# Layer B's scores of a pair of heads in one run of matmuls, in a two-layer attention encoder

## The chip, the cores and the metric

The kernel runs on one core of one Trainium2 chip. The metric is the device time of one execution, in microseconds; lower is better. TensorE is called PE here, VectorE DVE, ScalarE ACT, GpSimd POOL, and the queue of SyncE, which issues nearly all transfers, SP.

## The reference

Two layers work on 512 tokens of width 1024, in float32. Each layer normalises its input, projects it (q, k, v and a gate), attends with 16 heads of 64, multiplies by the SiLU of the gate, projects back and adds the input. Layer A is a dilated sliding-window attention; layer B, the one that the change touches, attends over a grid of 8 rows by 64 columns:

```python
def mixer_b(hn, w_in, w_out, q_gain, k_gain, rpb):
    proj = hn @ w_in
    q, k, v, gate = jnp.split(proj, 4, axis=-1)
    q = rms_norm(q.reshape(b, s, N_HEADS, HEAD_DIM), q_gain) * (HEAD_DIM ** -0.5)
    k = rms_norm(k.reshape(b, s, N_HEADS, HEAD_DIM), k_gain)
    ...
    def row(r):                      # one of 8 grid rows; 4 blocks of 16 columns
        ...
        logits = jnp.einsum('bhcqd,bhrcjd->bhcqrj', qr, kr).astype(jnp.float32) + bias
        logits = jnp.where(col_valid[:, :, None, :], logits, NEG_INF)
        p = jax.nn.softmax(logits.reshape(b, N_HEADS, n_cb, NA_COL_BLOCK, wr * NA_SLAB), axis=-1)
        ...
        out = jnp.einsum('bhcqrj,bhrcjd->bhcqd', p, vr)
    ...
    y = y * jax.nn.silu(gate)
    return y @ w_out
```

A query sees the keys of all rows in a slab of columns around its own. Each layer's output is added to its input.

## The kernel before

**Main work and side work.** PE's order is written out by hand. `main()` is a generator of the projections: weights stream in from memory, 512 KB at a time (`wraw`, three buffers, loaded by SP at L184), are split by ACT (`wh`, L132) and by DVE or POOL (`wl`, L138) into two parts of a reduced float32 type, and each product is made of three matmuls (high by high, high by low, low by high) of 512 columns into a PSUM bank of `acc` (four banks, `ps_acc`). `side()` is a second generator: attention, head pair by head pair. `run` takes a step of the main work (three matmuls, mostly), then lets the side work go on if it is due. What is due is kept on a clock of the kernel's own, which is counted as the program is written out, not on the chip: `matmul` adds 213 for 512 columns, so a step of three is 640; a transposition of 128 columns adds 109. `yield 1200` in the side work means "go on once the clock has gone 1200 further"; `later_on(9000, job)` puts a job in the program at the first step that is 9000 or more later. PE follows this order; ACT, DVE, POOL and SP are ordered by a scheduler that follows the program's order and a simulated timeline, except where `keep_in_program_order` pins an instruction. Instructions wait for each other's data by semaphores.

**The order of layer B's main work** is a list of parts: q and k of two pairs of heads at a time ("qk", moved by DVE and ACT into `raw` when a projection ends, L485), v of four pairs at a time ("v", into `rawk`, L485), and gates of one pair each. A "qk" or "v" part takes 96 full matmuls and needs all four `acc` banks, a gate 24 and one bank.

**Layer B's side work, `side_b(hc)`,** is done for eight pairs of heads (hc, or pair, 0 to 7). It asks for PSUM banks from a second pool of four (`bank`, `ps_side`), in turn:

1. For pairs 2 to 7, the P·V product of the pair before last (`pending`, `weigh`, tile `o`), whose P has been on its way through memory.
2. Bias rows for a later pair (`bias_b`, SP L748 and L753, tile `eb`, two buffers).
3. q transposed on PE (bank `tp`), split into `qh` and `ql`; 2500 of the clock later k, split into `kh` (ACT, L661) and `kl` (DVE, L665).
4. 1750 later the scores. There are four blocks of 128 queries against 256 keys. `scores(u)` does two of them, u = 0 and then u = 1, into two banks `log`, one for each head of the pair: per block three products for each head. A head has 64 channels, so a matmul uses 64 of PE's 128 rows, and the two heads' matmuls go in pairs side by side. One call is 12 matmuls of 256 columns.
5. `softmax(hd, u, lg)` for each head and half: DVE adds the bias and takes the minimum (L1109; scores are kept negated) from `log` into `p`, ACT takes the exponential and its sum (L1119), DVE the reciprocal (L693), ACT scales (L694). The small tile `mn`, which carries minimum and sum, has four buffers; a call of `softmax` uses two, one for each block, from the minimum to the scaling.
6. P is transposed. For pairs 0 to 5 (`far`) DVE transposes squares of 32 (L770, tile `tr`); then SP writes `tr` to memory (`td<-tr`, L779) and reads it back in four parts, rearranged (`pt<-td`, L783). `turner.send` is called through `later_on` some time after the transpositions, and puts the four reads on the clock itself: 9500 after the send, and then 1200 apart. For pairs 6 and 7 PE transposes P in four turns 1000 apart, and `weigh` follows at once.

Between `scores(0)` with its softmax and `scores(1)` there is `yield 1200`, in which PE does main work.

Of the kernel before, what the change touches and what calls it, by code (L numbers as in the profile page):

```python
# [46 lines left out]
def tile_hybrid_encoder(  # L47
# [23 lines left out]
    def sb(t, off, dims):  # L71
        return bass.AP(t.tensor, t.offset + off, [t.ap[0]] + dims)
# [13 lines left out]
    def bank(name):  # L86

        return ps_side.tile([P, 512], F32, tag="side", name=name)
# [137 lines left out]
    def mm3_heads(os, lh, ll, rh, rl, last):  # L226

        for n, (l, r) in enumerate(((lh, rh), (lh, rl), (ll, rh))):
            for hd in range(2):
                hs = slice(64 * hd, 64 * hd + 64)  # L230
                matmul(os[hd], l(hs), r(hs), share=2, start=(n == 0), stop=(last and n == 2))
# [3 lines left out]
    def later_on(delay, job):  # L235

        timers.append((clock[0] + delay, job))
        timers.sort(key=lambda t: t[0])
# [452 lines left out]
    def normalise(pr, mn):  # L691

        nc.vector.reciprocal(mn[:, 3:4], mn[:, 2:3])  # L693
        nc.scalar.activation(pr, pr, AF.Copy, scale=mn[:, 3:4])  # L694

    def put_y(hc, o, permuted, last):

        gt, rest = st.pop(("gate", hc))
        for _ in rest:
            pass  # L700
        if last and permuted:
            for c in range(4):
                q = slice(P * c, P * c + P)
                of = lambda t: t.rearrange("p (s x) -> p s x", x=16)[:, :, 4 * c : 4 * c + 4]
                nc.vector.tensor_mul(of(gt), of(gt), of(o))
                src = gt.rearrange("p (t ja x) -> p x ja t", t=4, ja=8)[:, 4 * c : 4 * c + 4]
                h, l = (t[:, hc, q].rearrange("p (x ja t) -> p x ja t", x=4, ja=8) for t in (st["y_h"], st["y_l"]))
                nc.scalar.copy(h, src)
                nc.vector.tensor_sub(l, src, h.bitcast(F32))
            return  # L710
        h, l, src = st["y_h"][:, hc, :], st["y_l"][:, hc, :], gt
        if permuted:

            tc.keep_in_program_order(nc.vector.tensor_mul(gt, gt, o))
            src = gt.rearrange("p (t ja x) -> p x ja t", t=4, ja=8)
            h, l = (t.rearrange("p (x ja t) -> p x ja t", t=4, ja=8) for t in (h, l))
        else:
            for grid, line in ((mid_rc, mid_o), (edge_rc, edge_o)):
                nc.vector.tensor_mul(grid(gt), grid(gt), line(o))
        nc.scalar.copy(h, src)  # L720
        (nc.vector if last else nc.gpsimd).tensor_sub(l, src, h.bitcast(F32))
        stamp["ya" if permuted else "yb", hc, "y"] = 0
# [327 lines left out]
    def side_b(hc):  # L1050
# [27 lines left out]
        pt, turners = pq[:, 2048 * (hc % 2) : 2048 * (hc % 2) + 2048], []  # L1078
# [1 line left out]
        at = lambda a, hd, i: 448 * a + 224 * hd + 32 * i  # L1080

        def scores(u):
            lgs = [bank("log") for _ in range(2)]
            for b in (2 * u, 2 * u + 1):
                if b < 3:
                    m = lambda t_, hs: t_[hs, P * b : P * b + 256]
                else:
                    m = lambda t_, hs: sb(t_[hs], 0, [[384, 2], [1, P]])
                qs = slice(P * b, P * b + P)
                o = 256 * (b % 2)  # L1090
                mm3_heads(
                    [lg[:, o : o + 256] for lg in lgs],
                    lambda hs: qh[hs, qs], lambda hs: ql[hs, qs], lambda hs: m(kh, hs), lambda hs: m(kl, hs), True,
                )
            return [(hd, u, softmax(hd, u, lgs[hd])) for hd in range(2)]

        def softmax(hd, u, lg):
            pr = wk.tile([P, 512], F32, tag="p", name="p", bufs=4)
            for b in (2 * u, 2 * u + 1):
                mn = wk.tile([P, 4], F32, tag="mn", name="mn", bufs=4)  # L1100
                o = 256 * (b % 2)
                if b < 3:
                    parts = ((slice(0, P), o),)
                    n, ec = 256, 0
                else:
                    parts = ((slice(0, 64), o), (slice(64, P), o + P))
                    n, ec = 128, 256
                for rows, c in parts:
                    nc.vector.tensor_tensor_reduce(  # L1109
                        out=pr[rows, o : o + n],  # L1110
                        in0=lg[rows, c : c + n],
                        in1=e[rows, hd, ec : ec + n],
                        scale=1.0,
                        scalar=3.0e38,
                        op0=ALU.add,
                        op1=ALU.min,
                        accum_out=mn[rows, 0:1],
                    )
                nc.scalar.activation(  # L1119
                    pr[:, o : o + n], pr[:, o : o + n], AF.Exp, bias=mn[:, 0:1], scale=-1.0, accum_out=mn[:, 2:3]  # L1120
                )
                normalise(pr[:, o : o + n], mn)
            return pr
# [9 lines left out]
        def weigh():  # L1133
            assert not any(t.left for t in turners)
            vb = st["vb", hc // 4]
            o = bank("o")
            mms = []


            for d, n, m, i, a in (  # L1140
                (64, 128, 0, 0, 0), (0, 64, 0, 6, 0), (192, 256, 2, 3, 0), (448, 64, 3, 6, 2),
                (64, 256, 1, 1, 0), (320, 128, 3, 5, 0),
            ):
                q = [[32, min(n // 32, 4)], [1, 32]]
                p = [[448, min(n // 32, 4)], [1, 32]]
                if n == 256:
                    q, p = [[P, 2]] + q, [[32, 2]] + p
                mms.append((
                    lambda t_, d=d, q=q: sb(t_, d, q),
                    lambda hs, m=m: vb[:, m, P * (hc % 4) + hs.start : P * (hc % 4) + hs.stop],  # L1150
                    lambda hd, p=p, i=i, a=a: sb(pt, at(a, hd, i), p),
                ))
            side_by_side(o, mms)
            return o

        held = []
        for u in range(2):
            held += scores(u)
            yield 1200 if u == 0 else 2400
        if far(hc):  # L1160
            turned = turner(448)
            turners.append(turned)
            for hd, u, pr in held:
                turned.put(pr, 512 if u == 0 else 384, 224 * hd + 128 * u)
            later_on(9000, partial(turned.send, pt[:, :1792], 9500, 1200))
            pending.append(lambda: put_y(hc, weigh(), False, False))
            return
        for args in held:
# [27 lines left out]
    def side():  # L1196
# [48 lines left out]
        for hc in range(NHC):  # L1245
            yield from side_b(hc)
# [100 lines left out]
```

## Time and profile before

| | |
|---|---|
| time, median of 3 runs | 845.8 us (845.26 to 847.01) |
| profiled execution, span | 843.7 us |
| profiled execution, a time of its own | not listed beside the span; the runs' median lies 2.1 us above it |
| granted TensorE clock | 1.000 |
| PE busy | 837.7 us, 5378 matmuls |
| DVE, ACT, POOL busy | 528.4, 427.8, 294.2 us |
| HBM | 109.11 MB read, 31.12 MB written |
| layer B's scores on PE | from 616.2 us to 802.8 us, 192 pairs of matmuls, 16 visits |

Rows of the timeline are: start in us, time in us, engine, line, operation, tile written `<-` tiles read, shapes, count, and in brackets how long the engine had been idle before it and what released it. Rows of the waits are: engine, what waited, `<-` for whom; total us, times, longest. Rows of the chain (the work that ended last, followed back) are: start in us, us, what. PEld is PE's loading of weights, which can run under a matmul. A matmul's time in a row includes its passage through the array; the pace is read from the starts. L215 is the line of the helper `matmul`, so the tile's name tells what is computed: `acc` the projections, `log` the scores, `tp` transpositions, `o` P·V.

### The profile page before, as it was taken

To read this page: it belongs to the slowest core of one execution; us is meant where nothing else is said; L and a number is where in the kernel's file an instruction comes from. 1 tells how busy PE (TensorE), PEld (TensorE's weight loads), DVE (VectorE), ACT (ScalarE), POOL (GpSimd) and SP (SyncE) were. 2 spreads that over 40 slices of the span, in tenths; PEclk is the share of its full clock that TensorE was granted. 3 is DMA by queue.
4 is the path that set the end of the run, shared out by engine and by line. 5 is a ranking of instruction groups with operands and counts; after the bars stand their busy time and mean duration, and the time that the engine had idled before them with its cause. 6 is when DMAs were issued, how large, how long until landed. Compare 5 with 4: busy or idle time off the path is not lost.

```text
span 843.7 us, 14965 instructions
## 1 busy us (share of the span) xinstructions
PE 837.7 (99%) x5378; PEld 676.3 (80%) x5378; DVE 528.4 (63%) x1371; ACT 427.8 (51%) x899; POOL 294.2 (35%) x432
## 2 busy tenths in 40 slices
PE   9999999999999999999999999999999999999998
PEld 7788888788788788788788787888878877777777
DVE  7354684684674674675674675447565777668653
ACT  7432653563553653652653564344366465664541
POOL 3352442452441541542532341121521625235211
PEclk9999999999999999999999999999999999999999
DMA  6345478378378278378276364164236546447323
GB/s 253 112 132 178 150 215 248 139 212 259 124 213 258 98 227 246 95 235 244 92 220 189 115 195 110 60 233 176 78 102 197 155 145 191 121 150 202 102 92 131
DMA packets 64218, 141.20 MB, mean 167 GB/s; under 512 B 5648, under 2 KB 23248, under 8 KB 64144
## 3 DMA queue, kind: packets, MB, share of 16 engines
q1 hardware_dynamic: 64000, 139.99, 54.0%
q8 instruction: 42, 0.69, 0.3%
q10 hardware_dynamic: 144, 0.26, 0.1%
q14 instruction: 32, 0.26, 0.1%
HBM read 109.11 MB, written 31.12 MB: 166 GB/s over the span
## 4 chain that ended last, share of the span: by engine, by line
PE 95%; DMA 2%; ACT 1%; DVE 1%; issue 0%; SPq 0%; ACTq 0%
PE acc L215 80%; PE log L215 5%; PE o L215 5%; PE tp L219 3%; DMA pt<-td 1%; DMA wraw<-in_w 1%; DVE hn_l L403 1%; ACT p L1119 1%; DMA x_all<-in_xt 0%; ACT p L694 0%; DVE pt L1017 0%; PE pa L215 0%; ACT raw L485 0%; PE pl L215 0%; PE pk L215 0%
## 5 line engine op out<-in xcount | busy, mean ns | idle before, releaser
L132 ACT CAST wh<-wraw 128x512 fp32r<-128x512 f32 (+1 forms) x259 | 158.3, 612 | 283.5 <-PE acc L215 246.0
L215 PE MATMUL acc<-wh,hn_h 128*128 128x512 f32 x704 | 282.4, 402 | 1.1 <-ACT hn_h L402 0.7
L215 PE MATMUL acc<-wh,hn_l 128*128 128x512 f32 x704 | 274.2, 390 | 0.0
L215 PE MATMUL acc<-wl,hn_h 128*128 128x512 f32 x704 | 274.1, 390 | 0.0
L138 POOL TENSOR_TENSOR wl<-wraw,wh 128x512 fp32r<-128x512 f32 (+1 forms) x104 | 135.2, 1300 | 366.1 <-ACT wh L132 344.5
L138 DVE TENSOR_TENSOR wl<-wraw,wh 128x512 fp32r<-128x512 f32 (+1 forms) x156 | 111.8, 717 | 146.4 <-ACT wh L132 145.3
L215 PEld LDWEIGHTS acc<-wh,hn_h 128*128 128x128 f32 x704 | 132.1, 188 | 35.8 <-issue 5.6
L215 PEld LDWEIGHTS acc<-wh,hn_l 128*128 128x128 f32 x704 | 132.2, 188 | 28.6
L215 PEld LDWEIGHTS acc<-wl,hn_h 128*128 128x128 f32 x704 | 132.4, 188 | 25.2 <-POOL wl L138 0.3
L215 PE MATMUL acc<-y,wh 128*128 128x512 f32 (+1 forms) x272 | 82.5, 387 | 0.0
L215 PE MATMUL acc<-hn_h,wh 128*128 128x512 f32 x192 | 76.1, 396 | 0.0
L215 PE MATMUL acc<-hn_h,wl 128*128 128x512 f32 x192 | 74.9, 390 | 0.0
L215 PE MATMUL acc<-hn_l,wh 128*128 128x512 f32 x192 | 74.8, 389 | 0.0
L694 ACT ACTIVATE p<-p,mn 128x512 f32<-128x512 f32 (+3 forms) x128 | 69.4, 585 | 0.6 <-DVE mn L693 0.2
L857 ACT ACTIVATE p<-p,mn 128x512 f32<-128x512 f32 (+1 forms) x64 | 44.8, 701 | 46.8 <-DVE mn L846 46.5
L291 DVE TENSOR_REDUCE ss<-sq 128x4 f32<-128x256 f32 (+1 forms) x96 | 48.3, 505 | 30.1 <-POOL sq L290 18.7
L770 DVE STREAM_TRANSPOSE tr<-p 128x512 f32<-128x512 f32 (+1 forms) x80 | 53.7, 683 | 12.3 <-ACT p L694 11.6
L215 PEld LDWEIGHTS acc<-y,wh 128*128 128x128 f32 x272 | 48.1, 189 | 9.6 <-issue 1.3
L215 PE MATMUL acc<-y,wl 128*128 128x512 f32 (+1 forms) x136 | 51.4, 378 | 0.0
L215 PEld LDWEIGHTS acc<-hn_h,wh 128*128 128x128 f32 x192 | 36.1, 188 | 8.0 <-issue 0.3
L215 PEld LDWEIGHTS acc<-hn_h,wl 128*128 128x128 f32 x192 | 36.0, 188 | 7.7
L215 PEld LDWEIGHTS acc<-hn_l,wh 128*128 128x128 f32 x192 | 36.1, 188 | 7.0
(143 smaller groups left out, 1041.1 us busy)
## 6 DMA issues: line engine op xcount, KB each, us to landing
wraw<-in_w SPq DMA_DIRECT2D x119, 512.0 KB
td<-tr SPq DMA_DIRECT2D x14, 1024.0 KB
pt<-td SPq DMA_DIRECT2D x56, 256.0 KB
qd<-rawq SPq DMA_DIRECT2D x6, 1024.0 KB
qt<-qd SPq DMA_DIRECT2D x24, 256.0 KB
td<-tr SPq DMA_DIRECT2D x6, 896.0 KB
pt<-td SPq DMA_DIRECT2D x24, 224.0 KB
e<-l_d SPq DMA_DIRECT2D x32, 112.0 KB
```

The costliest lines, as they stand in the source:

```text
L132: nc.scalar.copy(h, raw)
L138: eng.tensor_sub(l, raw, h.bitcast(F32))
L215: nc.tensor.matmul(o, l, r, **kw)
L219: nc.tensor.transpose(o, i, ident)
L291: nc.vector.tensor_reduce(ss[:, i * ns : (i + 1) * ns], sq.rearrange("p (a b) -> p a b", b=64), axis=AX.X, op=ALU.add)
L403: return nc.vector.scalar_tensor_tensor(l, xk, g, h.bitcast(F32), op0=ALU.mult, op1=ALU.subtract)
L694: nc.scalar.activation(pr, pr, AF.Copy, scale=mn[:, 3:4])
L770: nc.vector.transpose(dst, src[:, :n].rearrange("p (i b k) -> p i b k", b=4, k=32))
L857: nc.scalar.activation(row, row, AF.Exp, bias=mn[:, 1:2], scale=-1.0, accum_out=mn[:, 2:3])
L1119: nc.scalar.activation(pr[:, o : o + n], pr[:, o : o + n], AF.Exp, bias=mn[:, 0:1], scale=-1.0, accum_out=mn[:, 2:3])
```

## The change

`scores(u)` now only issues matmuls and leaves its two banks in a dictionary. Both halves' scores are called in a row, so that 24 matmuls into four `log` banks stand together in PE's order with no main work between them. The softmax of the first half is written behind both; then comes the `yield 1200` that stood between the halves, then the second half's softmax and the `yield 2400`. The clock at which the transpositions of P start is the same as before. For pairs 0 to 5 the send of P is put 8200 instead of 9000 behind that point; its reads follow the send at the same distances.

```diff
         def scores(u):
-            lgs = [bank("log") for _ in range(2)]
+            lgs = lgs_of[u] = [bank("log") for _ in range(2)]
             for b in (2 * u, 2 * u + 1):
...
-            return [(hd, u, softmax(hd, u, lgs[hd])) for hd in range(2)]
+
+        lgs_of = {}
...
         held = []
         for u in range(2):
-            held += scores(u)
+            scores(u)
+        for u in range(2):
+            held += [(hd, u, softmax(hd, u, lgs_of[u][hd])) for hd in range(2)]
             yield 1200 if u == 0 else 2400
         if far(hc):
...
-            later_on(9000, partial(turned.send, pt[:, :1792], 9500, 1200))
+            later_on(8200, partial(turned.send, pt[:, :1792], 9500, 1200))
```

## The prediction

> **What bounds the kernel now.** I read the page's busy times first, then the waits of PE, then the chain that ended last.
>
> ```profile
> PE   837.7 (99%) x5378; PEld 676.3 (80%) x5378; DVE 528.4 (63%) x1371; ACT 427.8 (51%) x899; POOL 294.2 (35%) x432
> PE o L215 <- DMA pt<-td: 0.8, 1, 0.8
> PE acc L215 <- ACT raw L485: 0.3, 1, 0.3
> 662.40 9.75 PE acc L215 x42
> ```
>
> TensorE is busy for 99% of the span, and it has only two recorded waits after layer B's scores begin: 0.8 us for a transfer of P and 0.3 us for an evacuation. (The other waits lie at the start and between the layers.) So the end moves if PE has less to do, or does it with fewer losses between instructions, or if these two waits change. A busy PE isn't PE at its peak, so I looked at starts, not at busy time. The last row gives the undisturbed pace: 42 matmuls of 512 columns in 9.75 us, 0.232 us each. Now one pair of heads, where its two score visits stand in PE's timeline:
>
> ```profile
> 615.91 0.40 PE L215 MATMUL acc<-wh,hn_l 128*128 128x512 f32 x1
> 616.24 0.39 PE L215 MATMUL log<-kh,qh 64*128 64x256 f32 x2
> 616.46 0.28 PE L215 MATMUL log<-kl,qh 64*128 64x256 f32 x2
> ...
> 616.93 0.28 PE L215 MATMUL log<-kh,ql 64*128 64x256 f32 x2
> 617.14 0.50 PE L215 MATMUL acc<-wh,hn_h 128*128 128x512 f32 x1
> 617.48 0.40 PE L215 MATMUL acc<-wl,hn_h 128*128 128x512 f32 x1
> ...
> 618.41 0.39 PE L215 MATMUL acc<-wh,hn_l 128*128 128x512 f32 x1
> 618.73 0.39 PE L215 MATMUL log<-kh,qh 64*128 64x256 f32 x2
> ...
> 619.63 0.50 PE L215 MATMUL acc<-wh,hn_h 128*128 128x512 f32 x1
> 619.97 0.39 PE L215 MATMUL acc<-wl,hn_h 128*128 128x512 f32 x1
> 616.24 0.19 PEld L215 LDWEIGHTS log<-kh,qh 64*128 64x128 f32 x2 [0.36 <-issue]
> 103.17 0.28 PE L215 MATMUL log<-k0h,q0l 64*128 64x256 f32 x2
> 103.29 0.25 PE L215 MATMUL log<-k0h,q0h 64*128 64x192 f32 x2
> ```
>
> A visit is six pairs of matmuls on half the array's rows (64*128). Inside it a pair follows a pair after 0.117 us (616.46 to 616.93 are four steps). From the start of the last full matmul before it (615.91) to that of the second behind it (617.48) pass 1.57 us. Two full matmuls (0.46) and six pairs (0.70) account for 1.16; the other 0.40 is lost at the two changes of shape, about 0.1 each at the last full matmul, the first pair, the last pair and the first full matmul. The weight row says why: the first score weights load only when PE gets there, after 0.36 us idle, while inside a run they load under the matmul before. The second visit (618.41 to 619.97) loses 1.56 - 1.16 = 0.40 as well. [...]
>
> **The change, part by part.** *One run instead of two.* The matmuls and weight loads stay the same in number; eight pairs of heads make one visit where they made two, so eight visits' changes of shape go: 8 x 0.40 = 3.2 us of PE. Does a run that goes on into two other banks pay again at the bank change? Layer A's scores do just that (the 256-column pairs end one couple of banks, the 192-column pairs start the next): 103.17 to 103.29, 0.12 us, the ordinary step. So nothing is paid back there.
>
> *Banks.* The order in which the four banks are asked for doesn't change, and the two that the second half takes last held the turned q and k, whose readers (kh, kl, qh, ql) the first half needs too. So scores(1) finds them free. No bank is asked for between the scores and the softmax.
>
> *The softmax does not come sooner.* Its second half isn't waiting for scores now:
>
> ```profile
> 750.02 0.42 DVE L1109 CUSTOM_DVE_ANT_0 p<-log,eb 128x256 f32<-128x256 f32 x1 [0.23 <-ACT p L694]
> 749.59 0.41 ACT p L694
> ```
>
> In pair 5 the second half's first DVE step is released by ACT's normalisation of the first half (the four buffers of mn), at 750.02; its scores began 2.49 us behind the first half's, as in the pair above (616.24 to 618.73), and weren't what it waited for. Scores that are ready 1.7 us earlier (they now start 0.8 behind) therefore move nothing on DVE or ACT; both go on in step with the first half's scores. That matters where PE, now 0.40 us sooner per pair, meets something that ACT does after the softmax:
>
> ```profile
> 621.74 0.67 ACT L485 ACTIVATE rawk<-acc,rs_n 128x512 f32<-128x512 f32 x1
> 622.46 0.19 PEld L215 LDWEIGHTS acc<-hn_h,wh 128*128 128x128 f32 x1 [0.22 <-ACT rawk L485]
> 703.63 0.68 ACT L485 ACTIVATE raw<-acc,rs_n 128x512 f32<-128x512 f32 x1
> 704.36 0.50 PE L215 MATMUL acc<-wh,hn_h 128*128 128x512 f32 x1 [0.29 <-ACT raw L485]
> 755.52 2.39 ACT L485 ACTIVATE raw<-acc,rs_n 128x512 f32<-128x512 f32 x4
> 756.32 0.42 PE L215 MATMUL acc<-hn_h,wh 128*128 128x512 f32 x1
> sum 28.66, ACT 27.01; mean ACT 9.00
> ```
>
> After pair 0 the next projection's weights load 0.05 us after the evacuation of its bank (621.74 + 0.67 = 622.41); after pair 3 PE already waits for it; after pair 5 the first evacuation ends near 756.20 (755.52 and its own 0.68, an estimate from 703.63) and PE starts 0.12 later. The last row is ACT's busy time in the three stretches from the first softmax step of pairs 0, 3 and 5 to these places: 27.01 of 28.66 us, so there is nowhere for it to gain much. So at three pairs the saving turns into a wait for ACT: about 0.35, 0.40 and 0.30, together 1.05. I take this in full; its bounds are 0 (ACT happens to be earlier) and 1.2. Pairs 1, 2 and 4 meet no evacuation that late, and pairs 6 and 7 turn P on PE:
>
> ```profile
> 783.73 1.48 ACT L694 ACTIVATE p<-p,mn 128x256 f32<-128x256 f32 x4
> 784.81 0.48 PEld L219 LDWEIGHTS tp<-ident,p 128*128 128x128 f32 x3
> ```
>
> Pair 6's third turn needs the first two of these four, ready about 784.47, 0.34 before its start; 0.40 sooner it waits 0.06.
>
> *P sent sooner.* The send moves 800 units of the kernel's own clock forward, in which a full matmul counts 213; so one or two steps of three matmuls, 0.7 to 1.4 us. The one wait of PE for P is pair 4's:
>
> ```profile
> 752.80 0.60 SPq L748
> 754.77 5.69 DMA wraw<-in_w
> 760.48 6.09 DMA pt<-td
> 759.94 0.35 SPq L184 DMA_DIRECT2D wraw<-in_w  x1
> 760.48 1.19 SPq L783 DMA_DIRECT2D pt<-td  x1
> 766.82 1.53 PE L215 MATMUL o<-pt,rawk 128*64 128x128 f32 x20 [0.76 <-DMA pt<-td]
> 731.36 5.68 PE acc L215 x24
> 746.05 0.95 PE log L215 x12
> SPq L748 <- DVE mn L1109: 32.8, 6, 8.1
> ```
>
> Three of its four reads are issued before the weight load of 759.94, the fourth behind it at 760.48, and that one ends the wait. I counted the clock over the chain's eight pieces from the first of the two PE rows to the second. From the turn (12 of the 24 matmuls in): 2560 for 12 matmuls, 1493 for o, 1280, 436 for a transposition, 2560, 436, 640. A send due at 9000 fires at 9405, one due at 8200 fires at 8329, before the second transposition. The fourth read follows 13100 later, on the steps of 640 counted from pair 5's turn at 15805: at 22845 before, at 21565 after. That is the very step at which the third read stood before, and so ahead of the weight load. Issued behind the third, near 757, it has over 3 us more and the 0.76 go. If it stays behind the load, all 0.76 stay.
>
> The send itself waits on SP for the last transposition into tr, and a weight load behind it would wait along. That costs nothing as long as the splits are ahead: the last row shows SP held up to 8.1 us by layer B's softmax (the bias loads of L748), and in that stretch PE shows no wait for weights. Leaving at most two steps sooner, a send can hold SP for 1.4 us more.
>
> **Sum.** 3.2 - 1.05 - 0.06 + 0.76 = 2.85 us. The profiled execution, with a span of 843.7, would be 840.85; the page gives no time of its own beside the span, and the median of the runs, 845.8, lies 2.1 above it. I keep that distance: 843.0.
>
> **Rivals.** *All eight visits pay.* ACT and DVE are ordered by a scheduler, and if it puts the evacuations a little further forward the 1.05 come back: 2.85 + 1.05 = 3.9, 841.9. For it speaks only that 3.2 are really taken off PE; against it that ACT is nearly full there. 0.10.
>
> *The fourth read stays behind the load.* SP's queue is ordered by the scheduler too. Then 2.1 remain: 843.7. My count speaks against it. 0.14.
>
> [...] 0.06.
>
> *Evacuations behind the softmax (slower).* The second half's scores are ready sooner, so the scheduler may queue its whole softmax on ACT ahead of the evacuations that now lie among it:
>
> ```profile
> 623.28 0.50 ACT L1119 ACTIVATE p<-p,mn 128x256 f32<-128x256 f32 x1
> 626.31 0.40 ACT L1119 ACTIVATE p<-p,mn 128x128 f32<-128x128 f32 x1
> 626.70 0.80 ACT L694 ACTIVATE p<-p,mn 128x256 f32<-128x256 f32 x2
> ```
>
> At pair 0 these are two of 0.50, two of 0.40 and twice 0.80, 3.4 us ahead of the bank that the gate needs at 622.50. At pair 3 between 0.7 (only the last scalings come ahead) and 2.4 (all that is left of the block). Together 4.1 to 5.8 against the sum: 847.0 to 848.7. It decides once ACT delays the bank by over 2.85 in total; a part of it (half the block at pair 0) ends at 844.7. [...] Against it: the softmax's place in the program is the same number of projection steps after the first scores, and its DVE steps are held by mn as before. 0.22, of which 0.10 for the full price.
>
> **How the numbers follow.** My case, 843.0, has 0.48. A measurement of this kernel can tell about 0.2%, 1.7 us, from no change: faster means under 844.1, slower above 847.5. Faster holds my case and the first two rivals, 0.72. Between lie the rule's rival and the partial delays, 0.18; slower is the full delay, 0.10. The range from 841.6 to 845.6 takes in all cases but the full delay and some of the edges.
>
> **What would show it.** Layer B's timeline of PE should hold eight score runs of 24 matmuls twelve pairs long, 0.117 us apart, about 1.6 us in the chain, with no full matmuls between; six full ones then follow before the softmax's second half is emitted, unseen on PE. PE's wait for pt should be gone and the fourth read should stand next to the third. "PE acc <- ACT raw" should have grown to near 1 us, at the projections' ends after pairs 0, 3 and 5. I am wrong if the waits for ACT stay at 0.3 (then it is faster than I say), if a step of over 0.2 us appears at the bank change, or if a new wait for weights or for P stands in the list.

## The result, and the profile after

| | before | changed |
|---|---|---|
| median of 18 runs each | 846.18 us (845.07 to 847.5) | 843.85 us (843.45 to 845.69) |
| ratio | 1 | 0.9977, 95% interval 0.997 to 0.9983 |
| span of the profiled execution | 843.7 us | 841.7 us |

The kernel became faster by 0.23%, which is 1.9 us (1.4 to 2.5). The forecast was 2.85 us of gain and 843.0 us. In some of the profiled executions the first matmuls run slower and all that follows is some 2 us later (the first twelve of the projections take 5.15 us with the merged scores alone, 5.25 to 10.40, and 2.86 in the changed kernel, 5.21 to 8.07), and by an estimate from the scatter of the runs (845.07 to 847.5 before) their medians move with how many of these they hold. So where pieces are compared below I take the stretch of layer B, from the start of its first transposition to that of its last P·V product: 610.40 to 813.00 before, 610.38 to 811.08 after, 1.90 us less.

PE's part of the page, and then its waits (columns: us, times, longest):

```profile
PE 835.7 (99%) x5378; PEld 676.3 (80%) x5378; DVE 528.1 (63%) x1371; ACT 427.9 (51%) x899; POOL 294.7 (35%) x432
PE acc L215 <- ACT rawk L485: 0.6, 1, 0.6
PE acc L215 <- ACT raw L485: 0.5, 2, 0.3
```

PE is busy for 2.0 us less with the same 5378 matmuls. The wait for pt has gone from the list; the waits for ACT's evacuations have grown from 0.3 to 1.1. Pair 0's visit in PE's timeline:

```profile
615.89 0.40 PE L215 MATMUL acc<-wh,hn_l 128*128 128x512 f32 x1
616.22 0.39 PE L215 MATMUL log<-kh,qh 64*128 64x256 f32 x2
...
616.91 0.29 PE L215 MATMUL log<-kh,ql 64*128 64x256 f32 x2
617.03 0.29 PE L215 MATMUL log<-kh,qh 64*128 64x256 f32 x2
...
617.62 0.29 PE L215 MATMUL log<-kh,ql 64*128 64x256 f32 x2
617.85 0.50 PE L215 MATMUL acc<-wh,hn_h 128*128 128x512 f32 x1
618.18 0.40 PE L215 MATMUL acc<-wl,hn_h 128*128 128x512 f32 x1
```

From 615.89 to 618.18 pass 2.29 us; two full matmuls (0.46) and twelve pairs (1.40) are 1.87 of them, and 0.42 is lost, once where 0.40 was lost twice. (All of layer B's scores are 192 matmuls, that is 96 such pairs, and not the 192 pairs of the table ahead.) The change into the other two banks (616.91 to 617.03) takes 0.12, the ordinary step. Now ACT behind that visit, in the kernel before (two rows) and in the changed one, and PE where it meets it:

```profile
620.54 1.29 ACT L694 ACTIVATE p<-p,mn 128x256 f32<-128x256 f32 x3
622.31 0.50 ACT L694 ACTIVATE p<-p,mn 128x256 f32<-128x256 f32 x1
...
620.01 1.29 ACT L694 ACTIVATE p<-p,mn 128x256 f32<-128x256 f32 x3
621.72 0.51 ACT L694 ACTIVATE p<-p,mn 128x256 f32<-128x256 f32 x1
622.13 0.66 ACT L485 ACTIVATE rawk<-acc,rs_n 128x512 f32<-128x512 f32 x1
622.84 0.50 PE L215 MATMUL acc<-hn_h,wh 128*128 128x512 f32 x1 [0.60 <-ACT rawk L485]
```

Before, three of the first half's four scalings stood ahead of the evacuation, which began at 621.74; now all four do, and it begins at 622.13. (ACT's casting of a weight tile, 0.60 us, which used to stand among the exponentials at 619.53, now stands among the scalings at 621.21.) PE, which is 0.40 sooner, waits 0.60. Next SP's queue, at the place of the former wait for P:

```profile
754.44 1.79 SPq L783 DMA_DIRECT2D pt<-td  x4
759.12 0.35 SPq L184 DMA_DIRECT2D wraw<-in_w  x1
```

All four reads of pair 4 now stand in one row ahead of the weight load. Last pair 6: k's split on DVE, the start of its scores on PE, of its softmax on DVE, ACT's scaling of the second half, the third turn that needs it, and PE's weight loads that waited for it (the 0.5 is this one; the other lies in layer A):

```profile
772.93 0.75 DVE L665 SCALAR_TENSOR_TENSOR kl<-tp,gk,kh 128x512 fp32r<-128x512 f32 x1 [0.68 <-ACT kh L661]
773.49 0.39 PE L215 MATMUL log<-kh,qh 64*128 64x256 f32 x2
773.74 0.39 PE L215 MATMUL log<-kl,qh 64*128 64x256 f32 x2
773.96 0.28 PE L215 MATMUL log<-kh,ql 64*128 64x256 f32 x2
775.98 0.41 DVE L1110 CUSTOM_DVE_ANT_0 p<-log,eb 128x256 f32<-128x256 f32 x1
782.82 1.48 ACT L694 ACTIVATE p<-p,mn 128x256 f32<-128x256 f32 x4
783.36 0.62 PE L219 MATMUL tp<-ident,p 128*128 128x128 f32 x3
PEld tp L219 <- ACT p L694: 0.7, 2, 0.5
```

The scores start 1.62 us sooner than before (775.11), the softmax only 0.91 (776.89): DVE does k's split and a projection's scaling first, and the split waits for ACT's part of k, which comes only 0.90 sooner (773.13 before, 772.23 now). PE now meets DVE and ACT twice. The scores' second pair needs k's split, which ends at 773.68, and the first two steps take 0.25 and 0.22 us where pair 0 has 0.22 and 0.12, 0.13 more. At the third turn PE runs into the second half's scaling, and the two steps from the second turn to the fourth take 3.92 us where they took 3.56, 0.36 more.

Where the 1.90 us came from can be read off PE's timeline at ten places, by how much sooner each comes than before. The column "foreseen" is the prediction's sum, taken apart.

| place (us before, us after) | gained since the place before | by | foreseen |
|---|---|---|---|
| tp of pair 0 (610.40, 610.38) | | | |
| tp of pair 1 (634.18, 634.54) | -0.38 | visit of pair 0 | 0.05 |
| o of pair 0 (660.64, 660.61) | 0.39 | visit of pair 1 | 0.40 |
| o of pair 1 (685.53, 685.09) | 0.41 | visit of pair 2 | 0.40 |
| o of pair 2 (715.48, 715.04) | 0.00 | visit of pair 3 | 0 |
| o of pair 3 (736.97, 736.13) | 0.40 | visit of pair 4 | 0.40 |
| gate behind pair 5 (756.32, 755.42) | 0.06 | visit of pair 5 | 0.10 |
| o of pair 4 (766.82, 765.19) | 0.73 | the wait for P | 0.76 |
| o of pair 6 (788.57, 787.03) | -0.09 | visit of pair 6 | 0.34 |
| o of pair 7 (813.00, 811.08) | 0.38 | visit of pair 7 | 0.40 |

### The profile page after: what moved, and what is told of

It is laid out like the page before. It is cut to its first block, busy times and chain, and to the rows that moved or that the text cites. A ratio compares the mean times of both kernels' runs of the same rounds, so it can differ in the third digit from the quotient of the medians.

```text
span 841.7 us, 14967 instructions
## 1 busy us (share of the span) xinstructions
PE 835.7 (99%) x5378; PEld 676.3 (80%) x5378; DVE 528.1 (63%) x1371; ACT 427.9 (51%) x899; POOL 294.7 (35%) x432
## 4 chain that ended last, share of the span: by engine, by line
PE 94%; ACT 2%; DVE 2%; issue 0%; DMA 0%; DVEq 0%; ACTq 0%
PE acc L215 80%; PE o L215 5%; PE log L215 5%; PE tp L219 3%; ACT p L1120 1%; ACT p L694 1%; DVE hn_l L403 1%; DMA x_all<-in_xt 0%; DVE raw L313 0%; DVE p L1110 0%; ACT wh L132 0%; ACT raw L485 0%; DVE wl L138 0%; DVE pt L1017 0%; PE pa L215 0%
```

## Experiments

Theory V is the one above: a visit costs PE 0.40 us in changes of shape, and where ACT or DVE is the later one, they keep it. Its rival O puts the gain down to the sooner send and the changed order on the other engines.

**The merged scores alone.**

```diff
-            later_on(8200, partial(turned.send, pt[:, :1792], 9500, 1200))
+            later_on(9000, partial(turned.send, pt[:, :1792], 9500, 1200))
```

> The changed kernel with the send of P back at 9000: only the merged scores. Theory V (a visit of the scores costs PE 0.40 us in changes of shape; what isn't refunded at pairs 0, 3, 5 and 6 is taken by waits for ACT and DVE): PE's wait for pt at pair 4's product is back at 0.8 us or a little more, pair 6 then keeps some 0.3 of its saving, so 1.3 to 1.7 us faster than before. Rival O (the gain comes from the sooner send and a luckier order on the other engines, the visits hardly count): within 0.4 us of before.

Measured: 847.72 us, ratio to before 1.0025 (1.0015 to 1.0036), so slower, and layer B takes 2.16 us longer than before. Both theories missed it. SP's queue and PE, and then the busy times with PE's granted clock (PE, PEld, DVE, ACT, POOL busy; clock; DMA share; GB/s):

```profile
707.66 1.32 SPq L783 DMA_DIRECT2D pt<-td  x3
711.79 0.35 SPq L184 DMA_DIRECT2D wraw<-in_w  x1
712.18 0.43 SPq L779 DMA_DIRECT2D td<-tr  x1
712.66 6.17 SPq L783 DMA_DIRECT2D pt<-td  x2
719.51 2.66 PE L215 MATMUL o<-pt,rawk 128*64 128x128 f32 x24 [2.30 <-DMA pt<-td]
719.50:722.00 2.50, 2.49 (x24) 1.63 (x24) 0.00 (x0) 0.00 (x0) 0.00 (x0) 0.64 0.99 299
722.00:724.00 2.00, 2.00 (x7) 1.57 (x6) 1.79 (x5) 0.18 (x1) 0.00 (x0) 0.60 0.46 117
```

Three of pair 2's reads stand at 707.66, the fourth behind a weight load and behind pair 3's write of 896 KB (712.18). Its data end PE's wait of 2.30 us, and the matmuls after it run at a granted clock of 0.64 and 0.60: the 24 of o take 2.66 us where they took 1.75, and by the next transposition 4.0 us are lost against the changed kernel, 1.6 of them behind the wait. By the kernel's clock the reason is the merge itself. No timer fires within a step of the side work; both halves' scores are now one step of 1280. From pair 2's turn to pair 3's scores PE has 30 full matmuls (6400 of the clock), one o (1493) and eight transpositions (872), together 8765. The send is due at 9000, so within the step, and comes out at 10045, where it came out at 9405 between the halves. Its reads follow one step later.

**Only pair 2's send sooner**, to tell that place from a general crowding of transfers.

```diff
-            later_on(8200, partial(turned.send, pt[:, :1792], 9500, 1200))
+            later_on(8200 if hc == 2 else 9000, partial(turned.send, pt[:, :1792], 9500, 1200))
```

> The changed kernel with the send at 8200 for pair 2 alone, 9000 for all others. The merged scores are one step of 1280 on the kernel's clock, in which no timer fires, and pair 2's send, due 9000 behind its turn, falls just into that step of pair 3 and so one step later than before; its fourth read then stands behind pair 3's write of 0.9 MB. Theory F (this one place made the merged scores alone slower): PE's wait at pair 2's product is gone, the small one at pair 4's (0.5 to 0.8) stays: 0.3 to 0.9 us slower than the changed kernel, over 3 us faster than the merged scores alone. Rival (the transfers of several pairs collide): at most 2 us faster than the merged scores alone.

Measured: 843.82 us, 0.9978 (0.9969 to 0.9988); layer B takes 0.62 us longer than in the changed kernel. Pair 2's four reads stand together ahead of pair 3's write again:

```profile
707.19 1.80 SPq L783 DMA_DIRECT2D pt<-td  x4
...
711.71 0.43 SPq L779 DMA_DIRECT2D td<-tr  x1
PE o L215 <- DMA td<-tr: 1.1, 1, 1.1
```

So one send at one pair was the whole loss, and the wait at pair 4's product (here 1.1; its fourth read stands at 761.12, behind a weight load again) is what the other sends bring. That the step of 1280 put pair 2's send there is worked out from the clock; that its place decides is shown. With that place mended layer B takes 1.28 us less than before: this is what the merged scores bring by themselves, at the lower end of the 1.3 to 1.7 that V gave them.

**The sooner send alone**, on the kernel before.

```diff
-            later_on(9000, partial(turned.send, pt[:, :1792], 9500, 1200))
+            later_on(8200, partial(turned.send, pt[:, :1792], 9500, 1200))
```

> The kernel before with only the send of P at 8200. V: the wait for pt (0.76) goes, the fourth read stands with the third ahead of a weight load; pair 6 gives up to half of it back, since its softmax doesn't come sooner by as much: 0.4 to 0.8 us faster than before. O: most of the 2 us, 1.5 or more.

Measured: 845.05 us, 0.9995 (0.9985 to 1.0004): by the runs not to be told from before. In its profile layer B takes 0.66 us less and PE has no wait for P, as V says. O is out: the send alone brings a third of the gain. Its 0.66 and the 1.28 of the merged scores make 1.94, close to the 1.90 of the change.

**Twice the visits**, on the kernel before.

```diff
                 mm3_heads(
                     ...
                 )
+                if b % 2 == 0:
+                    yield 600
...
-            held += scores(u)
-            yield 1200 if u == 0 else 2400
+            held += yield from scores(u)
+            yield 600 if u == 0 else 1800
```

> The kernel before with each half's scores split once more, one step of main work between the two blocks (yields shortened so that all later places on the kernel's clock stay): 32 visits instead of 16, the same matmuls. V: 16 x 0.40 = 6.4 us more on PE, less what the present waits at pairs 3 and 5 swallow (about 0.9 and 0.8) and with up to 1 added where the first half's softmax now starts 1.1 us later: 4.5 to 6.5 us slower than before; start to start 0.40 us over the content at each visit of three pairs. O: within 1 us of before.

Measured: 853.45 us, 1.0086 (1.0073 to 1.0099). By the runs this is 7.3 us (6.2 to 8.4), above the 4.5 to 6.5 foreseen; in the profile layer B takes 5.31 us longer, which lies within. Two visits of pair 1:

```profile
642.58 0.39 PE L215 MATMUL log<-kh,qh 64*128 64x256 f32 x2
642.80 0.28 PE L215 MATMUL log<-kl,qh 64*128 64x256 f32 x2
642.92 0.28 PE L215 MATMUL log<-kh,ql 64*128 64x256 f32 x2
643.13 0.50 PE L215 MATMUL acc<-wh,hn_h 128*128 128x512 f32 x1
643.47 0.40 PE L215 MATMUL acc<-wl,hn_h 128*128 128x512 f32 x1
643.70 0.39 PE L215 MATMUL acc<-wh,hn_l 128*128 128x512 f32 x1
644.02 0.39 PE L215 MATMUL log<-kh,qh 64*128 64x256 f32 x2
```

From visit to visit 1.44 us, of which three pairs (0.35) and three full matmuls (0.70) are 1.05: 0.39 lost, about 0.1 at each of four steps: the first pair's, the last pair's, the first full matmul's and the last one's. Sixteen more visits are 6.2 us. Of the 0.9 that is missing, 0.41 is at pair 3, where PE's wait for ACT has gone, and 0.40 at pair 4's product, where PE's wait for P has fallen from 0.76 to 0.43; pair 5, where I had foreseen another 0.8, swallowed nothing (its two visits cost 0.78). The price of a visit is shown.

**Pairs 0, 3 and 5 sooner**, so that ACT is done with their softmax when a projection ends.

```diff
-(1500, 23500, 12000, 31000, 8500, 23000)[hc - 2]
+(1500, 20500, 12000, 28000, 8500, 23000)[hc - 2]
...
-(12000, 33000, 12000, 26000, 17500, 33500, 11000, 26000)[hc]
+(9000, 33000, 12000, 23000, 17500, 30500, 11000, 26000)[hc]
```

> The changed kernel with the side work of pairs 0, 3 and 5 put 3000 of the kernel's clock (3.3 us) sooner, so that ACT is through with their softmax when a projection ends. V: PE's waits for ACT raw and rawk go (0.6 and 0.5 us, with exposed weight loads about 0.75 at pair 0, 0.9 at pair 3, 0.3 at pair 5): 1.4 to 2.0 us faster than the changed kernel, 3.3 to 4 faster than before. Rival R (ACT and DVE are so full there that the wait only moves to another place): under 0.5 us faster than the changed kernel.

Measured: 844.88 us, 0.9984 (0.9975 to 0.9993): no better than the changed kernel. Waits of PE, and SP's queue:

```profile
PE acc L215 <- ACT raw L485: 1.3, 2, 0.7
PE o L215 <- DMA pt<-td: 0.8, 1, 0.8
706.73 0.43 SPq L779 DMA_DIRECT2D td<-tr  x1
707.21 0.50 SPq L783 DMA_DIRECT2D pt<-td  x1
```

The wait at pair 0 is gone, but at pair 3 the scheduler ordered ACT anew and PE waits twice there, and pair 3's write, sooner as well, is back ahead of pair 2's last read. Moving pair 3 costs what the others bring: the next experiment, without it, starts pair 2's product 1.45 us sooner (714.25 against 715.70).

**Pairs 0 and 5 alone**: the same edit without pair 3 (23500 and 26000 kept).

> The changed kernel with the side work of pairs 0 and 5 alone put 3000 of the clock sooner, pair 3 left where it was (moving it turned the order of pair 3's write and pair 2's last read). V: PE's wait at pair 0 (0.75 with the exposed load) and at pair 5 (0.2 to 0.3) go, nothing else moves: 0.8 to 1.1 us faster than the changed kernel. Rival R (the waits only move): within 0.3 us of it.

Measured: 842.78 us, 0.9959 (0.9946 to 0.9972). Its span is 1.6 us under the changed kernel's. Of the waits for ACT one of 0.3 is left, at pair 3:

```profile
PE acc L215 <- ACT raw L485: 0.3, 1, 0.3
```

By the places of the table above pair 0 gives 0.80, pair 5 0.52 and pair 6 0.33 (its scores no longer wait for k's split, and the third turn starts 0.25 us behind the matmul ahead of it, 781.48 to 781.73, where it took 0.46 in the changed kernel, 782.90 to 783.36). That is more than the 0.8 to 1.1 foreseen, because pair 6 had not been counted. So ACT had indeed kept the saving at these pairs.

**More buffers of mn**, to see what held the second half.

```diff
-                mn = wk.tile([P, 4], F32, tag="mn", name="mn", bufs=4)
+                mn = wk.tile([P, 4], F32, tag=("mn", "mnb")[u], name="mn", bufs=4)
```

> The changed kernel with four further buffers of mn for the second half, so that its DVE steps needn't wait for ACT's scaling of the first half. Theory V (ACT is full at pairs 0, 3 and 5, and mn only keeps the second half behind): DVE's second half starts right behind the first, over 1 us sooner; ACT then has more softmax in front of the evacuations, so PE waits as long or longer for them: between 0 and 2 us slower than the changed kernel. Rival M (mn is what makes the softmax late, so the sooner scores would pay without it): 0.5 us or more faster than the changed kernel.

Measured: 850.73 us, 1.0047 (1.0031 to 1.0064); layer B takes 5.07 us longer than in the changed kernel. PE's waits, and ACT behind pair 0:

```profile
PE acc L215 <- ACT rawk L485: 2.4, 1, 2.4
PE acc L215 <- ACT raw L485: 1.8, 1, 1.8
PE tp L219 <- ACT p L694: 1.4, 1, 1.4
622.55 0.50 ACT L1120 ACTIVATE p<-p,mn 128x256 f32<-128x256 f32 x1
626.02 0.67 ACT L485 ACTIVATE rawk<-acc,rs_n 128x512 f32<-128x512 f32 x1
```

The second half's exponentials now start at 622.55, between the first half's scalings, and the evacuation that PE needs comes at 626.02. This is the prediction's slower rival, let loose. Four buffers of mn were what kept it away: they hold back work that ACT has no room for. It costs more than the 0 to 2 us foreseen: 3.4 of the 5.07 are lost at pair 0, 1.8 of them by the longer wait (2.36 where it was 0.60) and 1.6 because PE's full matmuls behind it start 0.43 us apart for a while and not 0.23, as the last section shows.

**q and k transposed in one run** of eight, on the changed kernel, as a test of the price in another place.

```diff
         tp = transpose4(raw, 0)
+        tpk = transpose4(raw, P)
...
-        yield 2500 if hc < NHC - 1 else 2000
-        tp = transpose4(raw, P)
-        put_k([(kh, kl, tp)], 3)
+        put_k([(kh, kl, tpk)], 3)
         stamp["qk", hc] = 0
-        yield 1750 if hc < NHC - 1 else 1250
+        yield 4250 if hc < NHC - 1 else 3250
```

> The changed kernel with q's and k's transpositions of a pair in one run of eight instead of two visits of four. V by the same reading (a visit of transpositions loses about 0.2 us at its changes of shape, from the starts around it): 8 x 0.2 = 1.6 us less on PE, of which pairs 0, 3 and 5 may give theirs to the wait for ACT: 0.8 to 1.6 us faster than the changed kernel. Rival (a run of transpositions isn't another shape, the visit costs nothing): within 0.3 us of it.

Measured: 842.39 us, 0.9961 (0.9948 to 0.9974); layer B takes 1.27 us less than in the changed kernel. The size came as expected, but not the terms: from the first transposition to the scores each pair gains only about 0.09 (pair 0: 612.15 to 617.90 against 610.38 to 616.22), 0.7 in all, and most of the rest is pair 6, whose earlier k lets its softmax be ready for the turns (from o of pair 4 to o of pair 6 PE takes 0.56 us less than in the changed kernel). A visit of transpositions loses less than half of what I had put.

**Both together.**

> Both gains together: the changed kernel with pairs 0 and 5 3000 of the clock sooner and q's and k's transpositions in one run. V: the two add up, since the one takes waits for ACT away and the other changes of shape: 2.2 to 3.2 us faster than the changed kernel, 4.2 to 5.2 faster than before. Rival (they share a limit, ACT or DVE): no faster than the better one of the two.

Measured: 841.1 us, 0.9935 (0.9922 to 0.9948), the fastest of all, 5.5 us under before. Layer B takes 0.97 us less than with the moved pairs alone; by the runs the interval just touches that of the one run of transpositions. The gain is less than the sum of the two, since both had counted pair 6's wait: from o of pair 4 to o of pair 6 PE takes 21.28 us here and with the one run alone, 21.51 with the moved pairs alone and 21.84 in the changed kernel.

**The P·V product next to the transpositions**, for pairs 3, 5, 6 and 7, on top of that.

```diff
-(1500, 23500, 12000, 28000, 8500, 23000)[hc - 2]
+(1500, 26000, 12000, 30500, 11000, 26000)[hc - 2]
...
             pending.pop(0)()
-            yield
+            if hc in (2, 4):
+                yield
```

> The same, and for pairs 3, 5, 6 and 7 the P.V product of an earlier pair put directly ahead of the transpositions, with no main work between: one change of shape from full matmuls and one back to them fewer for each, one between o and tp more. V: about 0.2 us each, 0.8 in all; 0.3 to 1.0 us faster than the kernel without it, unless the later o makes DVE late for q. Rival: within 0.3 us.

Measured: 842.3 us, 0.9952 (0.9937 to 0.9968), not faster; in the profile it takes 0.6 us longer from the first transposition to the end. At pair 3 PE waits 0.8 us for evacuations (0.3 without this edit) and then 0.2 for pair 2's P (none without it), new or larger waits that can eat the 0.8; which of the later o's brings them, and what takes the rest, stays open.

## Why the prediction was right, and where it wasn't

- **The price of a visit** held: 0.40 foreseen, 0.38 to 0.41 at the four pairs that nothing else limits, 0.39 in the kernel with twice the visits. The rival at 0.06, that the changes of shape are not saved, is out. The weights of a visit's first scores load only after the weight row has been idle for 0.36 us, before (616.24) as in the changed kernel (616.22). Whether these late loads alone make the 0.1 us lost at each of the four steps is separated by no run here.
- **The banks** cost nothing, 0.12 at the change.
- **The softmax came no sooner**, and mn was what held it. Right at pairs 1 to 5 and 7, where DVE's steps of the second half start at the same distance from the scores as before, and weightier than I put it: without that hold the change loses. At pair 0 they start 0.54 sooner (620.53 against 621.07), because ACT put a weight tile's cast behind the first scalings.
- **Pairs 3 and 5** kept their savings for ACT, as foreseen (0.00 and 0.06).
- **The wait for P** went by the step that the clock gave: 0.73 of 0.76.
- **The step that failed: "about 0.35" at pair 0.** I had ACT's order stand as it was, so that only the 0.40 could turn into a wait. But ACT also put one more scaling (0.4 us) ahead of the evacuation, so that the visit cost 0.38 net instead of giving 0.05. The rival "evacuations behind the softmax" happened there to about a tenth of its price. These 0.43 are half of what is missing.
- **The other: "0.40 sooner it waits 0.06" at pair 6.** I let the visit's 0.40 come sooner, but not the 0.76 of the vanished wait just ahead of it. DVE and ACT gave only part of that along, so PE waited for k's split (0.13) and at the third turn (0.36); of these 0.49 only 0.06 was foreseen, so 0.43 more is missing. Two runs bear this out: where the wait for P is left standing (the merged scores alone, and with only pair 2's send sooner), the same stretch takes 21.35 us against 21.75 before, and the visit gives its 0.40 in full. Together the two steps take 2.85 to 1.99; the other 0.09 is spread over the remaining places.
- **Unseen: what the sooner send was for.** I put it down as a gain of 0.76 at pair 4 and let the merge stand alone at 2.1. Alone it is slower by 0.25%, because it makes one step of the kernel's clock longer and turns the order of a read and a write on SP. I had worked the clock through for pair 4 and not for pair 2. So it is in part luck that the sum came near: the same send that I valued at 0.76 also kept pair 2's read ahead of pair 3's write, which is worth 3.4 us (layer B of the merged scores alone against that with pair 2's send sooner).

## What to carry to other kernels

Where the matmul engine is full (99% busy here), look at starts, not at busy time: a run of another shape can cost its changes in and out (0.40 us here), and runs that can stand together should. What was taken off that engine was kept here only where the others were ahead of it (0.41 us at pair 2, 0.00 at pair 3), so count for each place who is next; and an order written out on a clock of its own can shift at unexpected places when a step becomes longer (pair 2's send here, 3.4 us), so follow every transfer that falls due inside that step.

## What the runs showed of the hardware that I had not expected

A wait of PE of 0.76 us left no trace behind it, and neither did the waits of 1.41 and 1.82 us in the kernel with more buffers of mn: the granted clock of the stretches around and behind them is 1.00 (766 to 769 before; 700 to 740 and 780 to 830 with more buffers). The 2.30 us in the merged scores alone and the 2.36 us with more buffers of mn did leave one. With the merged scores alone the granted clock is 0.64 from the wait's end to 722.00, 0.60 to 724.00 and then 1.00; with more buffers of mn full matmuls start 0.43 us apart from 628.33 to 631.32, the first of them 1.58 us after the wait has ended (626.75), and from 631.65 on 0.23. Each time 1.6 us were lost after the wait had ended. The rows behind the waits of 2.36 and 1.82 us, the latter with no step of 0.43:

```profile
626.75 0.50 PE L215 MATMUL acc<-hn_h,wh 128*128 128x512 f32 x1 [2.36 <-ACT rawk L485]
...
628.33 0.63 PE L215 MATMUL acc<-hn_h,wh 128*128 128x512 f32 x1
628.76 0.63 PE L215 MATMUL acc<-hn_l,wh 128*128 128x512 f32 x1
...
708.15 0.50 PE L215 MATMUL acc<-wh,hn_h 128*128 128x512 f32 x1 [1.82 <-ACT raw L485]
708.48 0.39 PE L215 MATMUL acc<-wl,hn_h 128*128 128x512 f32 x1
708.71 0.40 PE L215 MATMUL acc<-wh,hn_l 128*128 128x512 f32 x1
```

These five gaps do not fix a limit: whether the length alone decides, or also when the gap falls, was not tried.

And a visit of transpositions lost only 0.09 us (pair 0, q's and k's in one run against two) where one of half-height matmuls lost 0.40.
